# Delta-rule sequences of a hybrid decoder trunk: state maps made ahead of the chunk chain

## The chip, the cores and the metric

The kernel runs on one core of a Trainium2 chip. Its measure is the device time of one execution in microseconds (us), lower being better. The profile comes from one execution taken by the hardware profiler. Engines are named PE (TensorE, the matrix products), DVE (VectorE), ACT (ScalarE), POOL (GpSimd) and SP (SyncE, which here only issues DMAs).

## What is computed

The reference is a trunk of four layers over 1024 tokens of width 1024. Layers 0 and 3 are gated convolutions, layer 1 is a diagonal state-space layer, layer 2 is RWKV-7 time mixing. Each is followed by a gate and a layer norm. The change touches only layer 2, whose recurrence over time is, for each of 16 heads with a 64 x 64 state:

```python
def _rwkv_step(state, inp):
    r_t, w_t, k_t, v_t, kk_t, a_t = inp
    sa = jnp.einsum("bhvk,bhk->bhv", state, -kk_t)
    state = (state * w_t[:, :, None, :] + sa[..., None] * (kk_t * a_t)[:, :, None, :]
             + v_t[..., None] * k_t[:, :, None, :])
    out = jnp.einsum("bhvk,bhk->bhv", state, r_t)
    return state, out
# then: group norm of out over each head, times lnx_g plus lnx_b,
# plus a bonus sum(r*k*r_k)*v, times silu(z), times w_out
```

## The kernel before

All tensors of layer 2 lie transposed, 128 channels (two heads) on the partitions, and time is cut into two halves `h` of 512 tokens, each half into 8 chunks of 64. A block `m` (0 to 7) is one pair of heads. `rwkv_layer` runs, for each half, the z and v projections of all blocks, and then a loop over `m` (L1832 to L1863) that holds the recurrence in its chunked form. A projection of 512 columns is `mm3`: 24 products of 128x128 by 512 (L326 to L328).

The iteration of block `m` is made of generators of `inner_setup`: `use_k` and `use_r` (the scaled vectors: `kb` on the one side, `ra` on the other, `ant` the transposed half of `ra`, all per chunk), `prep` (the chunk-internal products, L1982, masked; `kb` scaled and transposed to `kbt`, L2001 to L2009; a product `wps` with v, L2017), `tsolve` (the triangular inverse on DVE, L2037 to L2054), `join` (its 32-blocks are put together to `tt`, L2063 to L2087, and applied to `ant`, L2097) and `seq` (the chain over the 8 chunks, and then norm and output).

In `seq`, `bank` (L2117 to L2123) first adds the v part of two chunk pairs into a PSUM bank `p1`. Then each chunk takes four steps that hang on each other: a PE product of `ra` with the state into `p1` (L2131), an ACT copy of the 64 result rows to `uv` (L2132), a PE product of `kbt` with `uv` into `p2` (L2137), and two DVE operations of 64x64 which decay the state and add the two diagonal blocks of `p2` (L2140). After chunks 3 and 7 the outputs are finished (L2147, L2150). The state is 128x128 with two 64x64 blocks in use. The norm (eight ACT squares L2162, POOL L2163 and L2169), four transposes back `otp` (L2176) and the last two POOL products (L2180, L2181) end `seq`.

Some 18 PSUM tiles per block rotate through `aux`, a pool of two banks. `p1` has two banks, `sq` (for `p2` and `otp`) one. Tiles from `slot(S, tag, ...)` share 16 buffers per tag: in the second half `tt`, `ant`, `uv`, two `scr` and two `kbt` of each block come from one such set.

What is issued when: the program is traced in the order of the generators' pulls (`pull(inner, IP)` takes `seq` of the block before last in pieces), and a scheduler then orders each engine's instructions by priority. `prio` moves `join` and `prep` ahead by 600 and `seq` and `tsolve` by 300. `issue_after(x)` keeps the PE instructions of a block behind `x`. Each engine then runs its list in that fixed order.

Of the kernel before, what the change touches and what calls it, by code (L numbers as in the profile page):

```python
# [15 lines left out]
P = 128  # L16
# [1527 lines left out]
PS, PT, PJ = 300, 300, 600  # L1544

# [52 lines left out]
def rwkv_layer(S, X, bg, l, last, nxt):  # L1598
# [9 lines left out]
    dST = dram_list(S, "dST", [P, P])  # L1608
# [182 lines left out]
    for h in range(2):  # L1791
# [38 lines left out]
        with S.tc.issue_after(act_set.ins):  # L1830
            Rs = [Ctx() for _ in range(NB)]
            for m in range(NB):  # L1832
# [47 lines left out]
            inner.append(prio(I.seq(NB - 1, h, Rs[NB - 1], dVT, dST, dBV, dZ, dY), PS))  # L1880
# [41 lines left out]
def inner_setup(S, rg, T_):  # L1922
# [35 lines left out]
    G.memset(zero, 0.0)  # L1958

    def prep(m, h, R):  # L1960
# [41 lines left out]
        R.kbt = []  # L2002
        for g in range(2):
            ps = aux("kbtp")
            for i in range(4):
                nc.tensor.transpose(ps[:, i * P:(i + 1) * P], kb[:, 4 * g + i, :], S.ident)
            t = slot(S, ("a0", "a1")[h], "kbt")
            SC.copy(t, ps)
            R.kbt.append(t.rearrange("p (a b) -> p a b", a=4))  # L2009
            yield  # L2010

        pss = [aux("wps"), aux("wps")]
        for c in range(4):
            for hd in range(2):
                for w in range(2):
                    rb, rk = rows_b[w], rows_k[w]
                    nc.tensor.matmul(pss[w][rb, c * P + hd * 64:c * P + hd * 64 + 64], sca[rk, w, c, hd, :],  # L2017
                                     R.uv[w][rk, c, hd * 64:hd * 64 + 64], start=True, stop=True)
# [3 lines left out]
        yield  # L2022

# [33 lines left out]
    def join(m, h, R):  # L2057
# [24 lines left out]
        for e in range(8):  # L2082
            for w in range(2):
                nc.tensor.matmul(ps[w][q0[w], e * 32:(e + 1) * 32], zs[q1[w], e, :], tt[q1[w], e, 32:64],
                                 start=True, stop=True)
# [6 lines left out]
        ps = [aux("a2"), aux("a2")]  # L2092
        for c2 in range(4):
            for hd in range(2):
                for w in range(2):
                    rb = rows_b[w]
                    nc.tensor.matmul(ps[w][hd * 64:hd * 64 + 64, c2 * CH:(c2 + 1) * CH],  # L2097
                                     an[rb, c2, hd * 64:hd * 64 + 64], tt[rb, 2 * c2 + hd, :], start=True, stop=True)
        for w in range(2):
            SC.copy(r5[:, :, w, acol[w]], ps[w][:, 0:256].rearrange("p (c t) -> p c t", c=4))  # L2100
# [4 lines left out]
    def seq(m, h, R, dVT, dST, dBV, dZ, dY):  # L2105
        st = rg.tile([P, P], F32, tag="state", name="state", bufs=2)
        if h == 0:
            G.memset(st, 0.0)
        else:
            nc.sync.dma_start(st, dST[m][:])  # L2110
        ot = rg.tile([P, HT], F32, tag="o", name="o", bufs=2)
        o4 = ot.rearrange("p (c s) -> p c s", c=4)

        def bank(ph):

            p1 = S.pseq.tile([P, 2, 2, P], F32, tag="p1", name="p1", bufs=2)
            nc.tensor.matmul(p1[:, 0, 0, 0:2], S.ident, zero, start=True, stop=False, skip_group_check=True)  # L2117
            for c2 in range(2):
                for hd in range(2):
                    for w in range(2):  # L2120
                        rb, cs = rows_b[w], slice(hd * 64, hd * 64 + 64)
                        nc.tensor.matmul(p1[rb, w, c2, cs], R.tt[rb, 2 * (2 * ph + c2) + hd, :],
                                         R.uv[w][rb, 2 * ph + c2, cs], start=False, stop=False, skip_group_check=True)  # L2123
            return p1
        p1s = [bank(0)]
        for c in range(8):
            w, c2, ph = c % 2, c // 2, c // 4
            rb = rows_b[w]
            uv = R.uv[w][:, c2, :]
            p1 = p1s[ph][:, w, c2 % 2, :]  # L2130
# [3 lines left out]
            if c == 2:  # L2134
                p1s.append(bank(1))
            p2 = sq("p2")
            last = nc.tensor.matmul(p2[:, 0:P], R.kbt[c // 4][:, c % 4, :], uv, start=True, stop=True)  # L2137
            for hd in range(2):
                cs = slice(hd * 64, hd * 64 + 64)
                V.scalar_tensor_tensor(st[cs, cs], st[cs, cs], R.pc[cs, c:c + 1], p2[cs, cs], ALU.mult, ALU.add)  # L2140
            if c % 4 == 3:
                with S.tc.issue_after(last.ins):
                    for k in range(2):
                        for hd in range(2):
                            for w in range(2):
                                cs = slice(hd * 64, hd * 64 + 64)
                                nc.tensor.matmul(p1s[ph][rows_k[w], w, k, cs], R.scr[w][:, 2 * ph + k, hd, :],  # L2147
                                                 R.uv[w][:, 2 * ph + k, cs], start=False, stop=True, skip_group_check=True)
                for w in range(2):
                    SC.copy(o4[rows_k[w], 2 * ph:2 * ph + 2, :], p1s[ph][rows_k[w], w])  # L2150
            yield
        if h == 0:
            nc.sync.dma_start(dST[m][:], st)
# [59 lines left out]
```

## Time and profile before

| | |
|---|---|
| time, median of 3 runs | 2817.57 us (2812.04 to 2817.90) |
| profiled execution | 2819.03 us, its span 2817.1 us |
| mean granted PE clock | 0.966 |
| PE, DVE, ACT, POOL busy | 95%, 71%, 41%, 23% of the span |

The shares are means over very different stages. The loop over the blocks of layer 2 lies, for the first half, from about 1290 to 1620 us after the span's start, and for the second from about 1745 to 2020 us; the chain of the last block of each half runs on into the stage behind it. In those stretches an engine's row in a timeline shows each instruction's start, its duration and, in brackets, the idle time before it with the engine and tile that ended it. Durations of PE rows overlap, since matmuls are pipelined: what one costs is read from start to start.

### The profile page before, as it was taken

What the parts mean: (1) busy time and instruction counts of PE and PEld (TensorE: products, weight loads), DVE (VectorE), ACT (ScalarE), POOL (GpSimd) and SP (SyncE); (2) the same over time, 40 slices, a digit from 0 to 9 for tenths busy, and PEclk for the clock granted to TensorE, in tenths of its full rate; (3) what the DMA queues carried; (4) which work ended last, traced back from release to release, by engine and by line L of the source; (5) the groups of instructions that cost most, each with busy time, mean ns of one, the idle gap of its engine ahead of it and who ended that gap; (6) DMA issues with size and microseconds to landing.
All of it is one profiled execution on the core that took longest, in us unless ns stands there. A gap on an engine that the chain in (4) does not pass through costs nothing.

```text
span 2817.1 us, 40692 instructions
## 1 busy us (share of the span) xinstructions
PE 2673.0 (95%) x14939; PEld 2119.2 (75%) x14939; DVE 2009.8 (71%) x3584; ACT 1168.8 (41%) x2243; POOL 644.9 (23%) x696
## 2 busy tenths in 40 slices
PE   8999999999999999899899899888889999999998
PEld 6887888778887878677677567666668777887887
DVE  6787865477657446887887776888866678877544
ACT  3333332242135223666565475555433343224332
POOL 1143422221115132203243110333222211111000
PEclk9999999999999999999996799999799999999999
DMA  5333321347774233473222245223324433324511
GB/s 169 99 97 98 94 76 58 92 146 211 217 237 157 90 101 102 134 227 120 77 95 91 60 163 168 76 85 93 100 91 135 139 115 116 101 72 131 172 64 38
DMA packets 463129, 331.56 MB, mean 118 GB/s; under 512 B 49449, under 2 KB 398929, under 8 KB 462929
## 3 DMA queue, kind: packets, MB, share of 16 engines
q1 hardware_dynamic: 462928, 328.96, 38.5%
q8 instruction: 118, 1.93, 0.3%
q14 instruction: 83, 0.67, 0.1%
HBM read 250.77 MB, written 77.59 MB: 117 GB/s over the span
## 4 chain that ended last, share of the span: by engine, by line
PE 71%; DVE 15%; issue 4%; ACT 4%; DMA 3%; POOL 3%; SPq 0%; DVEq 0%; POOLq 0%; ACTq 0%
PE op L327 3%; PE op L326 3%; PE op L328 3%; PE gp L328 3%; PE gp L327 3%; PE gp L326 3%; PE sp L326 2%; PE sp L327 2%; PE sp L328 2%; PE qa L506 2%; PE qa L507 2%; PE qa L508 2%; DVE tv L2048 2%; PE zp L326 2%; PE zp L328 2%
## 5 line engine op out<-in xcount | busy, mean ns | idle before, releaser
L299 DVE TENSOR_TENSOR wl<-wraw,wh 128x1024 fp32r<-128x1024 f32 x255 | 332.6, 1304 | 217.0 <-ACT wh L298 213.5
L298 ACT CAST wh<-wraw 128x1024 fp32r<-128x1024 f32 x255 | 267.4, 1049 | 519.0 <-PE gp L327 185.9
L905 POOL TENSOR_TENSOR ln_s<-ln_s,rp 128x512 f32<-128x512 f32 x42 | 60.3, 1435 | 209.9 <-DVE rp L901 209.9
L2140 DVE SCALAR_TENSOR_TENSOR state<-state,pc,p 64x64 f32<-64x64 f32 x256 | 70.8, 277 | 39.7 <-PE p L2137 35.5
L2048 DVE TENSOR_TENSOR tv<-ti,mi 128x128 f32<-128x128 f32 (+3 forms) x128 | 97.1, 759 | 2.5
L2131 PE MATMUL p<-state,ra 128*128 128x128 f32 x256 | 65.2, 341 | 31.3 <-DVE state L2140 31.0
L2131 PEld LDWEIGHTS p<-state,ra 128*128 128x128 f32 x256 | 45.2, 213 | 54.8 <-DVE state L2140 49.2
L2132 ACT COPY uv<-p 64x128 f32<-64x128 f32 x128 | 33.3, 260 | 122.2 <-PE p L2131 121.0
L920 POOL TENSOR_TENSOR rp<-r_0h,r_0l 128x512 f32<-128x512 f32 x24 | 36.5, 1548 | 180.9 <-PE op L327 180.2
L328 PE MATMUL gp<-r_0h,wl 128*128 128x512 f32 x192 | 77.2, 402 | 0.0
L327 PE MATMUL gp<-r_0l,wh 128*128 128x512 f32 x192 | 76.8, 400 | 0.0
L326 PE MATMUL gp<-r_0h,wh 128*128 128x512 f32 x192 | 76.6, 399 | 0.0
L326 PE MATMUL gp<-r_1h,wh 128*128 128x512 f32 x192 | 76.4, 398 | 0.0
L328 PE MATMUL gp<-r_1h,wl 128*128 128x512 f32 x192 | 76.0, 396 | 0.2 <-DVE wl L299 0.2
L327 PE MATMUL gp<-r_1l,wh 128*128 128x512 f32 x192 | 75.5, 393 | 0.0
L2137 PE MATMUL p<-uv,kbt 128*128 128x128 f32 x256 | 66.2, 344 | 8.7 <-ACT uv L2132 8.6
L1982 PE MATMUL s<-ra,kb 64*128 64x128 f32 x512 | 71.6, 302 | 1.0 <-ACT scr L1988 0.9
L2137 PEld LDWEIGHTS p<-uv,kbt 128*128 128x128 f32 x256 | 44.9, 210 | 36.6 <-ACT uv L2132 31.3
L1982 PEld LDWEIGHTS s<-ra,kb 64*128 64x128 f32 x512 | 61.3, 202 | 13.4 <-ACT scr L1988 2.9
L1991 POOL TENSOR_TENSOR scr<-scr,mask 128x512 f32<-128x512 f32 x32 | 45.9, 1435 | 70.2 <-ACT scr L1988 70.0
L327 PE MATMUL sp<-xs0l,wh 128*128 128x512 f32 x128 | 55.0, 430 | 1.9 <-DVE xs0l L195 1.9
L1710 POOL COPY pc<-pt 128x8 f32<-128x8 f32 x16 | 5.5, 342 | 222.0 <-ACT pt L1707 222.0
(851 smaller groups left out, 8734.7 us busy)
## 6 DMA issues: line engine op xcount, KB each, us to landing
wraw<-in_conv_w_in_dram SPq DMA_DIRECT2D x84, 512.0 KB
wraw<-in_rwkv_w_rkvz_dram SPq DMA_DIRECT2D x64, 512.0 KB
wraw<-in_ple_gate_dram SPq DMA_DIRECT2D x56, 512.0 KB
wraw<-in_conv_w_out_dram SPq DMA_DIRECT2D x24, 512.0 KB
xt<-xd SPq DMA_DIRECT2D x48, 256.0 KB
wraw<-in_ssm_w_in_dram SPq DMA_DIRECT2D x21, 512.0 KB
xd<-rp SPq DMA_DIRECT2D x40, 256.0 KB
wraw<-in_rwkv_w_out_dram SPq DMA_DIRECT2D x16, 512.0 KB
```

Of the source, the lines that this page charges most:

```text
L298: nc.scalar.copy(wh, raw)
L299: nc.vector.tensor_tensor(wl, raw, f32(wh[:]), ALU.subtract)
L326: nc.tensor.matmul(ps, lh, xh, start=(n == 0), stop=False)
L327: nc.tensor.matmul(ps, lh, xl, start=False, stop=False)
L328: nc.tensor.matmul(ps, ll, xh, start=False, stop=(n == kt - 1))
L506: nc.tensor.matmul(ps, wh[:, k0 + k, :], xh, start=first and k == 0, stop=False, skip_group_check=True)
L905: nc.gpsimd.tensor_tensor(s, s, rs, ALU.add)
L1982: nc.tensor.matmul(pss[hd][:, c * P:(c + 1) * P], kb[rows, 2 * c + w, :], ra[rows, 2 * c + w, :], start=True, stop=True)
L2048: V.tensor_tensor(tv, ti[:, b:8, 4 * b:4 * b + 4].unsqueeze(2).to_broadcast([P, n, c, 4]), mi[:, 4 * b:4 * b + 4, 0:c].rearrange("p q c -> ...
L2131: nc.tensor.matmul(p1, R.ra[:, c, :], st, start=False, stop=False, skip_group_check=True)
L2137: last = nc.tensor.matmul(p2[:, 0:P], R.kbt[c // 4][:, c % 4, :], uv, start=True, stop=True)
L2140: V.scalar_tensor_tensor(st[cs, cs], st[cs, cs], R.pc[cs, c:c + 1], p2[cs, cs], ALU.mult, ALU.add)
```

## The change

Only layer 2's `prep`, `join`, `seq` and the way they are queued are changed.

- `join` makes, besides the `ra` columns, `at` (16 products of 64x64 with an ACT copy) and from it, with `kbt`, a map `G` per chunk, written by 4 ACT copies into the diagonal blocks of a zeroed 128x128 tile (`gbd`, two buffers).
- `seq` makes both `p1` banks at once, copies them to `uv`, adds `kbt`·`uv` for all chunks into one bank `pd` (16 products of 128x64), and then a chunk's step is one PE product of `G` with the state (now 128x64) and one DVE operation. The states of all chunks are kept; `diag` spreads four of them into a block-diagonal tile, and `queries`, `to_uv` and `outs` make the outputs of four chunks together. In the second half the last step is left out.
- The squares of the norm become one ACT operation and one DVE reduction. The norm is a generator `tail` of its own.
- The transposes back and what follows are a generator `back`, traced one block later, without raised priority, its transposes (now in `aux`) kept behind the PE products of the next `join`.
- In `prep`, the transposes to `kbt` come behind the `wps` products.

```diff
@@ rwkv_layer, in the loop over m (and the same after it for the last block)
                 if m > 0:
                     for _ in prio(I.join(m - 1, h, Rs[m - 1]), PJ):
                         pass
-                    inner.append(prio(I.seq(m - 1, h, Rs[m - 1], dVT, dST, dBV, dZ, dY), PS))
+                    if m > 1:
+                        inner.append(I.back(m - 2, h, Rs[m - 2], dBV, dZ, dY, Rs[m - 1].joined))
+                    inner.append(prio(I.seq(m - 1, h, Rs[m - 1], dST), PS))
+                    inner.append(prio(I.tail(m - 1, Rs[m - 1]), PS))
@@ prep: kbt behind wps
+            with S.tc.issue_after(last.ins):
+                for i in range(4):
+                    nc.tensor.transpose(ps[:, i * P:(i + 1) * P], kb[:, 4 * g + i, :], S.ident)
@@ join
+        R.joined = last.ins
+        with S.tc.issue_after(last.ins):
+            pa = aux("at")
+            for c2 in range(4):
+                for hd in range(2):
+                    for w in range(2):
+                        rb = rows_b[w]
+                        nc.tensor.matmul(pa[rb, c2 * P + hd * 64:c2 * P + hd * 64 + 64], tt[rb, 2 * c2 + hd, :],
+                                         an[rb, c2, heads[hd]], start=True, stop=True)
...
+        SC.copy(at.rearrange("p c s -> p (c s)"), pa)
...
+                    nc.tensor.matmul(pg[w][heads[hd], c2 * CH:(c2 + 1) * CH], at[rb, c2, heads[hd]],
+                                     R.kbt[c2 // 2][rb, (2 * c2 + w) % 4, heads[hd]], start=True, stop=True)
         for w in range(2):
+            for hd in range(2):
+                SC.copy(g5[heads[hd], :, w, heads[hd]], pg[w][heads[hd], 0:256].rearrange("p (c t) -> p c t", c=4))
@@ seq
+        pd = sq("pd")
+        clear(pd[:, 0:2])
         for c in range(8):
+            for hd in range(2):
+                nc.tensor.matmul(pd[heads[hd], c * CH:(c + 1) * CH], R.kbt[c // 4][:, c % 4, heads[hd]],
+                                 R.uv[c % 2][:, c // 2, heads[hd]], start=False, stop=False, skip_group_check=True)
...
+        def chain(c):
+            col = pd[:, c * CH:(c + 1) * CH]
+            nc.tensor.matmul(col, R.g[:, c, :], sv[:, c, :], start=False, stop=True, skip_group_check=True)
+            V.scalar_tensor_tensor(sv[:, (c + 1) % 8, :], sv[:, c, :], R.pc[:, c:c + 1], col, ALU.mult, ALU.add)
+
+        def diag(ph):
+            for hd in range(2):
+                SC.copy(sbd[heads[hd], :, heads[hd]], sv[heads[hd], 4 * ph:4 * ph + 4, :])
...
-            nc.tensor.matmul(p1, R.ra[:, c, :], st, start=False, stop=False, skip_group_check=True)
-            SC.copy(uv[rb, :], p1[rb, :])
-            last = nc.tensor.matmul(p2[:, 0:P], R.kbt[c // 4][:, c % 4, :], uv, start=True, stop=True)
-            for hd in range(2):
-                V.scalar_tensor_tensor(st[cs, cs], st[cs, cs], R.pc[cs, c:c + 1], p2[cs, cs], ALU.mult, ALU.add)
+        for c in range(8):
+            if c < 7 or h == 0:
+                chain(c)
+            if c == 3:
+                diag(0)
+            elif c == 4:
+                queries(0)
+            elif c == 5:
+                to_uv(0)
+            elif c == 6:
+                outs(0)
@@ tail, back
-        for g in range(8):
-            SC.activation(gsq[:, g, :], o[:, g, :], AF.Square, scale=0.125, accum_out=s2[:, g:g + 1])
+        SC.activation(gsq, o, AF.Square, scale=0.125)
+        V.tensor_reduce(s2, gsq, mybir.AxisListType.X, ALU.add)
-        ps = sq("otp")
+        ps = aux("otp")
+        with S.tc.issue_after(behind) if behind else ExitStack():
```

## Rows read from the trace of the kernel before

**Rows 1.** Busy time of one period: window, its length, then PE, PEld, DVE, ACT, POOL (instructions).
```profile
1897.20:1934.70 37.50, 32.45 (x341) 24.77 (x339) 33.70 (x77) 22.17 (x64) 13.98 (x14) 1.00 0.28 87
```
**Rows 2.** PE timeline and chain that ended last: a chain's first product, its last, the next chain's first.
```profile
1877.52 0.49 PE L2131 MATMUL p<-state,ra 128*128 128x128 f32 x2
...
1904.83 0.27 PE p L2131 x2
...
1915.03 0.49 PE L2131 MATMUL p<-state,ra 128*128 128x128 f32 x2
```
**Rows 3.** DVE timeline: the first operation of the next join.
```profile
1868.86 1.09 DVE L2063 STREAM_TRANSPOSE tt<-ti 128x256 f32<-128x256 f32 x2
```
**Rows 4.** What PE waited for, 1820 to 1960 us: total us, times, longest.
```profile
PE p L2131 <- DVE state L2140: 11.2, 8, 2.1
PE otp L2176 <- POOL o L2169: 3.8, 4, 1.0
PE kbtp L2006 <- POOL kb L2001: 3.5, 3, 1.2
```
**Rows 5.** PE timeline: pairs and small tiles between the projections.
```profile
1867.18 0.38 PE L2131 MATMUL p<-state,ra 128*128 128x128 f32 x2
1867.32 0.47 PE L326 MATMUL sp<-xs1h,wh 128*128 128x512 f32 x1
1867.63 0.39 PE L327 MATMUL sp<-xs1l,wh 128*128 128x512 f32 x1
1867.91 0.49 PE L2137 MATMUL p<-uv,kbt 128*128 128x128 f32 x2
1868.33 0.69 PE L2147 MATMUL p<-uv,scr 128*64 128x64 f32 x16
1868.94 0.50 PE L328 MATMUL sp<-xs1h,wl 128*128 128x512 f32 x1
1869.28 0.39 PE L326 MATMUL sp<-xs1h,wh 128*128 128x512 f32 x1
1869.51 0.39 PE L327 MATMUL sp<-xs1l,wh 128*128 128x512 f32 x1
...
1911.76 0.73 PE L2097 MATMUL a<-tt,ant 64*64 64x64 f32 x31
...
1912.33 0.80 PE L2122 MATMUL p<-uv,tt 64*64 64x64 f32 x21
```
**Rows 6.** Groups by line: busy us, mean ns (L1693 instead: ns min/median/max).
```profile
L2140 DVE SCALAR_TENSOR_TENSOR state<-state,pc,p 64x64 f32<-64x64 f32 x58 | 15.9, 274 | 3.5 <-PE p L2137 2.9
...
L1693 DVE TENSOR_REDUCE vsum<-vt x16: 683/692/693, 1236.3 to 1733.8; 128x8 f32<-128x512 f32 x16
...
L2132 ACT COPY uv<-p 64x128 f32<-64x128 f32 x30 | 7.8, 259 | 35.3 <-PE p L2131 35.1
L2162 ACT ACTIVATE gsq<-o 128x64 f32<-128x64 f32 x28 | 6.9, 247 | 0.1
L2150 ACT COPY o<-p 64x256 f32<-64x256 f32 x14 | 5.1, 367 | 2.4 <-PE p L2147 2.2
...
L2008 ACT COPY kbt<-kbtp 128x512 f32<-128x512 f32 x8 | 4.3, 590 | 2.3 <-PE kbtp L2006 2.3
```
**Rows 7.** What the SP queue waited for, 1820 to 1960 us.
```profile
SPq L2171 <- POOL yt L2180: 5.1, 4, 1.3
```
**Rows 8.** End of the first half: windows as in Rows 1, then PE's waits 1510 to 1670 us.
```profile
1580.00:1590.00 10.00, 6.14 (x85) 4.18 (x84) 8.93 (x23) 4.73 (x10) 2.75 (x2) 1.00 0.35 86
...
1610.00:1620.00 10.00, 10.00 (x88) 5.62 (x88) 1.13 (x3) 4.46 (x18) 0.24 (x1) 0.50 0.16 41
...
PE p L2131 <- DVE state L2140: 8.6, 9, 2.6
PE p L2137 <- ACT uv L2132: 6.4, 12, 1.6
```
**Rows 9.** PE's longest wait at the end of layer 2, 2040 to 2180 us.
```profile
PE otp L2176 <- POOL u L528: 8.0, 1, 8.0
```

More of the change, by code (lines that the diff above doesn't have):

```diff
@@ L1879, in rwkv_layer @@
                 pass
-            inner.append(prio(I.seq(NB - 1, h, Rs[NB - 1], dVT, dST, dBV, dZ, dY), PS))
+            inner.append(I.back(NB - 2, h, Rs[NB - 2], dBV, dZ, dY, Rs[NB - 1].joined))
+            inner.append(prio(I.seq(NB - 1, h, Rs[NB - 1], dST), PS))
+            inner.append(prio(I.tail(NB - 1, Rs[NB - 1]), PS))
+            inner.append(I.back(NB - 1, h, Rs[NB - 1], dBV, dZ, dY, None))
     def resid(r, m, h, ps):
@@ L1958, in inner_setup @@
     G.memset(zero, 0.0)
+    heads = [slice(hd * 64, hd * 64 + 64) for hd in range(2)]
+    gbd = [rg.tile([P, 8, P], F32, tag=f"gbd{i}", name=f"gbd{i}") for i in range(GB)]
+    sbd = rg.tile([P, 4, P], F32, tag="sbd", name="sbd")
+    for t in (*gbd, sbd):
+        G.memset(t, 0.0)
     def prep(m, h, R):
@@ L2022, in prep @@
         yield
+        R.kbt = []
+        for g in range(2):
+            ps = aux("kbtp")
+            with S.tc.issue_after(last.ins):
+                for i in range(4):
+                    nc.tensor.transpose(ps[:, i * P:(i + 1) * P], kb[:, 4 * g + i, :], S.ident)
+            t = slot(S, ("a0", "a1")[h], "kbt")
+            SC.copy(t, ps)
+            R.kbt.append(t.rearrange("p (a b) -> p a b", a=4))
+            yield
     def tsolve(R):
@@ L2083, in join @@
             for w in range(2):
[L2084 to L2085 removed]
+                last = nc.tensor.matmul(ps[w][q0[w], e * 32:(e + 1) * 32], zs[q1[w], e, :], tt[q1[w], e, 32:64],
+                                        start=True, stop=True)
         for w in range(2):
@@ L2101, in join, with seq, clear @@
         yield
     gn, bn = S.vec[("lnx_g",)], S.vec[("lnx_b",)]
-    def seq(m, h, R, dVT, dST, dBV, dZ, dY):
-        st = rg.tile([P, P], F32, tag="state", name="state", bufs=2)
+    def seq(m, h, R, dST):
+        sv = rg.tile([P, 8, CH], F32, tag="state", name="state", bufs=SVB)
         if h == 0:
-            G.memset(st, 0.0)
+            G.memset(sv[:, 0, :], 0.0)
         else:
[L2110 to L2114, printed above, removed]
+            nc.sync.dma_start(sv[:, 0, :], dST[m][:])
+        R.ot = rg.tile([P, HT], F32, tag="o", name="o", bufs=1)
+        o4 = R.ot.rearrange("p (c s) -> p c s", c=4)
+        def clear(cols):
+            nc.tensor.matmul(cols, S.ident, zero, start=True, stop=False, skip_group_check=True)
+        p1s = []
+        for ph in range(2):
@@ L2152, in seq, with to_uv @@
-        if h == 0:
-            nc.sync.dma_start(dST[m][:], st)
-        hs = slice(h * HT, (h + 1) * HT)
+                        rb = rows_b[w]
+                        nc.tensor.matmul(p1[rb, w, k, heads[hd]], R.tt[rb, 2 * (2 * ph + k) + hd, :],
+                                         R.uv[w][rb, 2 * ph + k, heads[hd]], start=False, stop=False, skip_group_check=True)
+            p1s.append(p1)
+        def to_uv(ph):
+            for w in range(2):
+                SC.copy(R.uv[w][rows_b[w], 2 * ph:2 * ph + 2, :], p1s[ph][rows_b[w], w])
@@ new lines, in seq, with tail @@
+        for c in range(8):
[9 more added lines that the diff above has]
+                outs(0)
+            yield
+        diag(1)
+        if h == 0:
+            nc.sync.dma_start(dST[m][:], sv[:, 0, :])
+        queries(1)
+        to_uv(1)
+        yield
+        outs(1)
+        yield
+    def tail(m, R):
+        ot = R.ot
@@ L2169, in seq, with back @@
         G.tensor_tensor(o, o, bcs(s1), ALU.mult)
+        yield
+    def back(m, h, R, dBV, dZ, dY, behind):
+        ot, hs = R.ot, slice(h * HT, (h + 1) * HT)
         bv = S.tmp.tile([P, HT], F32, tag="ln_s", name="bv", bufs=1)
@@ L2183, in seq @@
         yield
-    I.prep, I.tsolve, I.join, I.seq = prep, tsolve, join, seq
+    I.prep, I.tsolve, I.join, I.seq, I.tail, I.back = prep, tsolve, join, seq, tail, back
     return I
```

81 lines of the change are left out of this document (37 added, 44 removed).

## The prediction, made before the changed kernel ran

> **What bounds the kernel now.** I read the page's 40 slices first, to find layer 2; then the windows table over single periods of its loop, the timelines of PE and DVE in one of them, the waits of PE, and the chain that ended last. In the middle of the second half the loop repeats itself every 37.5 us. In such a period no engine is full: PE is busy 32.45 us and DVE 33.7 us of 37.5, ACT 22.2 and POOL 14.0 [rows 1]. So neither engine's work alone sets the period. The chain does. Its first product starts at 1877.52 and its eighth at 1904.83; the next chain begins at 1915.03, 37.51 us after the first [rows 2]. That makes 27.3 us for seven steps (3.9 us each) and 10.2 us from the last product to the next chain's first, in which the next `join` runs. One period earlier it is the same: the last L2131 starts at 1867.18, the last L2137 at 1867.91, and the join's first DVE operation at 1868.86 [rows 3, 5]. The join follows the end of the previous chain because of buffers: its `tt` comes from 16 slots shared with the `kbt` of three blocks, and the last L2137 is what still reads one. So chain and join form a loop: chain, `kbt` free, join, next chain. What PE loses in it stands in its waits over 140 us, that is 3.73 periods: 11.2 us before L2131 for the state, 3.8 before the transposes back, 3.5 before the transposes of `kb` [rows 4]; per period 3.0, 1.0 and 0.94, together 4.95, which with 32.45 busy gives 37.4.
>
> **The change, part by part, for one period.**
>
> *The loop is cut.* `kbt` is read by `pd` at the start of `seq` and not at each step, so its slots are free a chain earlier and `join` no longer waits for the chain's end. A step loses an ACT copy (259 ns), one PE pair and one of two DVE operations (274 ns) [rows 6]. I therefore take the 37.5 us loop to go, and ask what the engines' own work allows then.
>
> *PE work.* A product here is two instructions. A pair among projections costs between 0.14 us (1867.18 to 1867.32) plus the 0.08 by which the next projection product comes later (0.31 instead of 0.23), that is 0.22, and 0.42 us ahead of a small-tile run (1867.91 to 1868.33) [rows 5]; I take 0.30, nearer the first since most pairs stand among projections. Small tiles: the 16 of L2147 take 0.61 us to the next start, 0.038 each; L2097, whose tiles alternate over all four quadrants, 0.57 us for 32 (1911.76 to 1912.33), 0.018 each; L2122, which uses two quadrants, 0.80 for 21, 0.038 [rows 5].
> - Removed: 8 pairs L2137, 8 x 0.30 = 2.4.
> - Kept: 8 pairs on `ra`, now in two runs of four at about 0.22 instead of 0.30 plus: -0.6, of which I count 0.3, because four pairs still stand at the ends of runs.
> - `at`: out rows and in rows belong to the same chunk parity, two quadrants as in L2122, 32 x 0.038 = 1.2. `gt`: four quadrants as in L2097, 0.57. `pd`: 32 of 128x64 as in L2147, 1.2. One more clearing product: at most a pair, 0.14.
> - `G` times the state: 8 pairs (7 in the second half) with 64 instead of 128 moving columns. The trace has no such form; it lies between two L2147 instructions (0.08) and a pair ahead of a switch (0.42). I take 0.26, 2.1 in all, nearer to the 128x128 pair because the weights are as wide.
> - Interruptions: a projection product after one is spaced 0.31 to 0.34 instead of 0.23 [rows 5]. Before, some 18 of them come from L2131, L2137 and L2147; after, some 12. Six times 0.08: -0.5.
>
> Sum: 1.2 + 0.57 + 1.2 + 0.14 + 2.1 - 2.4 - 0.3 - 0.5 = +2.0 us. PE has 34.45 us of work in a period.
>
> *DVE work.* Eight of sixteen state operations go, 8 x 0.274 = -2.2; one 128x512 reduction comes, 0.69 [rows 6]: -1.5, so 32.2 us. *ACT work.* Out: 8 copies of 0.26 and 8 squares of 0.25, -4.1. In: one 128x512 copy (0.59), one square taken at the same 0.59, and 4 + 8 + 4 copies of 64x256 for `gbd`, `to_uv` and `diag` at 0.37 [rows 6], +7.1. Net +3.0, 25.2 of 37.5: covered, but ACT's copies now stand inside `join`.
>
> *Waits of PE.* The 1.0 us before the transposes back goes: they come a join later, when their input is long done. The 0.94 before `kbt` goes: the `wps` run now stands in that gap. Of the 3.0 us before the chain's products I keep half: there are as many waits for DVE as before, behind the same DVE queue, but what PE waits for is one DVE operation instead of two, and the scheduler has more runs to put between. Bounds: 0 and 3.0. New: `at` and two `a2` want three tiles of a pool of two, and `gt` two more, so PE can stand behind an ACT copy twice; a copy is 0.37 to 0.59 and each comes with about as much of queue, so 0 to 1.8; I take 0.4, because the scheduler can fill the gap with projections.
>
> Period after: 34.45 + 1.5 + 0.4 = 36.3 us, 1.2 less. Of 16 blocks some 12 have a full period; 12 x 1.2 = -14 us.
>
> *What is moved.* `back` brings its two loads and its store on SP and two POOL products one block later. Their number stays; SP waits 5.1 us in four periods before these loads for their buffer [rows 7], behind which weight loads are queued, but these run two tiles ahead: no cost, or up to 1.3 us per block if a weight load comes late. `o` has one buffer instead of two; the next block's first output copy comes behind that `join` anyway.
>
> *End of the first half.* There the last tile solve and block 6's chain are nearly alone: PE is busy 6.14 of 10 us at 1580 and the clock is at half (0.50, that is 1.2 GHz) at 1610 [rows 8]. PE waits 8.6 us for the state and 6.4 us for `uv` between 1510 and 1670 [rows 8]. The second kind has no place in the new chain; of the first I keep half: -10.7. The 0.50 at 1610 to 1620, with PE busy all ten, would give back 5 us if the clock did not fall; it fell after the thin stretch. I count nothing for it, since the chain there stays latency-bound, and put it into the range.
>
> *End of layer 2.* The last block's transposes back hold PE for 8.0 us behind POOL [rows 9]. The chain ends earlier, but POOL's list is made by the scheduler: between 0 and -8, I take -5.
>
> Sum: -14 - 10.7 - 5 = -30 us against the profiled execution of 2819 us: 2789. The median of the runs shown is 1.5 us below that execution, so I say 2788.
>
> *A rule against it.* The projection product after an L2131 pair is late by 0.08 us although both are 128x128, and after the 128x64 run by 0.11 [rows 5]. The Trainium skill (TensorEngine Tiling (Array Packing), Key Properties) says that changing the tiling mode drains the engine, and that changing only the tile does not. By that, 128x128 pairs among 128x128 projections cost no drain, so gathering them saves nothing (the -0.5 falls), while `at`, `gt` and `pd` are three new runs with a switch at either end, 6 x 0.11 = 0.66. The row's 0.08 within one mode speaks against half of the rule; its 0.11 is in line with the other half.
>
> **The rivals.**
>
> *Small tiles pay at each switch.* By the same six switches of 0.11 and without the -0.5, PE has 35.6 us, the period is 37.5 and the 14 us fall: 2803. For it: the 0.11 is measured. Against it: `at` follows a small-tile run, so that some of the switches are shared.
>
> *PE becomes the bound and keeps its waits.* If the scheduler places each chain product as soon as its own model has the state ready, and DVE (33.7 of 37.5 busy) is later than that, PE stands at each of eight steps as it does now. Then the period is 34.45 + 3.0 + 1.8 = 39.25, 12 x 1.75 = +21; the end of the first half gives its 10.7, the end of the layer nothing: 2829. It decides against the change as soon as the waits left in a period pass 3.05 us. For it: DVE is nearly full, and its operations take their turn; the chain's waits are the largest item now. Against it: two of three items of wait are taken away by construction.
>
> *The loop isn't cut.* `seq` now takes both `p1` banks and the only `sq` bank from its start, so the next one can't begin before the last output copy. With step times near today's 3.9 us, 8 x 3.9 plus banks and outputs (about 6 us of runs and copies) is 37 us: the same period under another name. Only the ends then gain, and extra ACT work takes some back: 2814, between 2808 and 2820.
>
> *Resources alone.* If projections close up to 0.23, the waits fall under 1 us and the clock no longer drops: periods of 34.5, 12 x -3 = -36, ends -10.7 - 8, clock -6: 2758.
>
> **How the numbers follow.** Forecast (2775 to 2800): 0.36. Switches (about 2803): 0.12. Resources alone: 0.18. Loop not cut: 0.14, of which 0.04 is still faster. PE bound with its waits: 0.20. A measurement of this kernel tells 0.2% from no change, that is 5.6 us. Faster: 0.36 + 0.12 + 0.18 + 0.04 = 0.70. Same: 0.09. Slower: 0.21 with the loop's upper end. The range reaches from 2755, the last mentioned gain, to 2833, the slower rival with a margin; outside I leave 0.08 below and 0.08 above.
>
> **What would show it.** Right: in a period DVE's state operations number eight, PE's busy time rises to about 34 us, the waits before the transposes back and before `kbt` are gone, the chain's steps fall from 3.9 to 2 to 2.5 us, and `join` starts before the chain of the block before it has ended. Wrong: PE waiting 3 us or more for the new state operation or for the copies of `at` and `gt` (the slower rival); a new chain that begins right after the last output copy of the one before (loop not cut); projection products spaced as before (switches).

## The result, and the profile after

The changed kernel takes 2801.31 us (median of 15 runs, 2788.56 to 2808.62) beside 2815.30 us for the kernel before (15 runs, 2812.04 to 2820.98). The ratio is 0.9944 with an interval of 0.9929 to 0.9958: 14 us faster, where 30 were forecast. The profiled execution of after took 2808.62 us (span 2806.6, mean granted clock 0.976) and is the slowest of its 15; that of before took 2819.03 (span 2817.1, clock 0.966). The two spans are 10.5 us apart, and it is this difference that the traces have to explain.

**Where the time went, by landmarks.** The first join operation of block 0 and of block 7 in each half cuts both spans into the same five pieces. DVE timeline of before, then of after (start us, us, engine, line, operation):

```profile
1337.84 1.04 DVE L2063 STREAM_TRANSPOSE tt<-ti 128x256 f32<-128x256 f32 x2
...
2054.70 1.08 DVE L2063 STREAM_TRANSPOSE tt<-ti 128x256 f32<-128x256 f32 x2
```
```profile
1342.79 1.04 DVE L2077 STREAM_TRANSPOSE tt<-ti 128x256 f32<-128x256 f32 x2
...
2042.51 1.09 DVE L2077 STREAM_TRANSPOSE tt<-ti 128x256 f32<-128x256 f32 x2
```

The windows between these landmarks, of before and then of after, with the columns of [rows 1]: the loop of the first half, the piece between the halves, the loop of the second half.

```profile
1337.84:1604.25 266.41, 236.43 (x2195) 181.75 (x2195) 229.72 (x522) 150.72 (x420) 83.28 (x90) 0.86 0.27 83
1604.25:1794.24 189.99, 178.06 (x982) 133.29 (x982) 134.21 (x231) 118.07 (x232) 30.52 (x30) 0.92 0.44 140
1794.24:2054.70 260.46, 225.13 (x2224) 174.21 (x2225) 226.01 (x513) 143.36 (x408) 81.57 (x81) 0.91 0.30 90
```
```profile
1342.79:1597.86 255.07, 239.27 (x2901) 193.46 (x2901) 211.43 (x476) 172.06 (x388) 84.86 (x90) 0.95 0.29 85
1597.86:1794.08 196.22, 180.72 (x1059) 137.84 (x1060) 134.94 (x221) 120.17 (x217) 32.63 (x30) 0.93 0.44 138
1794.08:2042.51 248.43, 240.58 (x2864) 195.47 (x2864) 197.81 (x457) 162.32 (x370) 78.46 (x81) 0.92 0.28 88
```

The two loops gained 11.3 and 12.0 us. The rest lost: 5.0 before the first landmark (1337.84 to 1342.79), 6.2 between the halves, 1.7 after the last (762.4 to 764.1 us). The sum is -10.5, the difference of the spans.

The second half is the cleaner of the two, since its clock is nearly the same (0.91 and 0.92). PE's idle time there fell from 260.46 - 225.13 = 35.3 us to 248.43 - 240.58 = 7.9, and its busy time rose by 15.5: 27.5 less of waiting, paid for with 15.5 more of work. In the first half the clock rose from 0.86 to 0.95, so part of its 11.3 us is clock.

**Did a block get shorter?** The join changes its place within a block, so its landmarks can't tell. The transpose `mi`, the last DVE operation of `prep`, hangs on the same work of a block in both kernels. Windows from the `mi` of block 1 to that of block 7, six periods in each half, of before and then of after:

```profile
1330.87:1552.99 222.12, 203.11 (x1908) 158.50 (x1908) 191.58 (x433) 126.18 (x347) 77.29 (x81) 0.87 0.28 88
1787.34:2014.05 226.71, 195.29 (x1950) 152.26 (x1949) 196.65 (x440) 124.63 (x349) 78.04 (x77) 0.91 0.28 88
```
```profile
1334.87:1562.93 228.06, 214.50 (x2566) 174.00 (x2563) 185.56 (x423) 149.44 (x342) 81.16 (x85) 0.95 0.30 88
1786.05:2012.61 226.56, 219.15 (x2559) 178.37 (x2558) 180.44 (x412) 147.18 (x337) 76.75 (x79) 0.92 0.27 85
```

It did not. The twelve periods take 448.8 us before and 454.6 after. In the second half PE's idle time fell by 4.0 us a period (31.4 to 7.4 us in all) and its busy time rose by 4.0, so the mean period stays at 37.8. In the first half PE had only 3.2 us of idle time a period to lose, and 0.9 of it went. The whole gain lies around the periods: from block 7's `mi` of the first half to block 1's of the second, 234.4 us became 223.1, and from block 7's of the second to the end of the span 803.1 became 794.0. The start up to block 1 lost 4.0.

**One period.** Windows row of a period of after, against [rows 1]:

```profile
1897.00:1933.50 36.50, 35.75 (x436) 28.63 (x435) 28.39 (x68) 25.36 (x58) 13.06 (x15) 1.00 0.29 89
```

36.50 us against 37.50: PE is busy in all but 0.75. This period is at full clock; from `mi` to `mi` the six of the second half last 33.7 to 41.8 us. ACT is where the prediction put it (25.36, forecast 25.2), PE is over its forecast (35.75, forecast 34.45), DVE far under (28.39, forecast 32.2). PE timeline in it:

```profile
1903.05 1.08 PE L2113 MATMUL at<-ant,tt 64*64 64x64 f32 x29
...
1905.73 0.92 PE L2164 MATMUL p<-uv,tt 64*64 64x64 f32 x25
...
1907.27 0.68 PE L2134 MATMUL gt<-kbt,at 64*64 64x64 f32 x16 [0.62 <-ACT gbd L2138]
1907.93 0.34 PE L2179 MATMUL pd<-uv,kbt 128*64 128x64 f32 x4
...
1911.51 0.43 PE L2185 MATMUL pd<-state,gbd 128*128 128x64 f32 x2
...
1918.24 0.43 PE L2185 MATMUL pd<-state,gbd 128*128 128x64 f32 x2
```

Six chain steps take 6.73 us, 1.12 each, against 3.9 in [rows 2]; in the other chains of this half a step takes 1.1 to 1.8. The DVE timeline shows what the join follows instead:

```profile
1895.06 2.08 DVE L2012 STREAM_TRANSPOSE mi<-dg 128x1024 f32<-128x1024 f32 x1 [1.38 <-ACT dg L2008]
1897.05 1.09 DVE L2077 STREAM_TRANSPOSE tt<-ti 128x256 f32<-128x256 f32 x2
...
1931.57 2.06 DVE L2012 STREAM_TRANSPOSE mi<-dg 128x1024 f32<-128x1024 f32 x1 [1.38 <-ACT dg L2008]
1933.55 1.08 DVE L2077 STREAM_TRANSPOSE tt<-ti 128x256 f32<-128x256 f32 x2
```

Twice the join's `tt` follows the `mi` of the next block's `prep` at once, where in [rows 3] it came behind the end of a chain. Behind it stand the join's products, the chain and the next block's scores, whose diagonal blocks give the next `mi`. What PE waited for, 1820 to 1960 us as in [rows 4] (total us, times, longest):

```profile
PE pd L2185 <- DVE state L2186: 1.9, 1, 1.9
PE gt L2134 <- ACT gbd L2138: 1.8, 4, 0.6
```

18.5 us of waits have become 3.7. The waits of [rows 8] are gone alike: between 1500 and 1680 us PE waits for the state 1.3 us instead of 8.6, and the 8.0 of [rows 9] has become 0.7. A new one stands between the halves, before a projection product (PE's idle time in that whole piece rose from 11.9 to 15.5 us):

```profile
PE sp L326 <- DVE sg L1663: 5.3, 1, 5.3
```

**The clock.** Of one program, 15 runs of after lie between 0.976 and 0.986, and the time follows: a straight line through them falls 19.3 us per 0.01 of clock (correlation -0.97); 25 runs of before on one chip give 19.4 (-0.89), other sets of its runs 15 to 19. Before has a median clock of 0.968 to 0.970, after of 0.980. That difference by that slope is 19 to 23 us, more than the 14 won. At an equal clock of 0.975 the two lines give some 2803 us for before and 2812 for after. This is an estimate beyond the runs of either line (those 25 have clocks of 0.967 to 0.972, after's 0.976 to 0.986), and the granted clock is itself a consequence of what a kernel puts on PE; but it made a second question: did the maps gain the time, or the clock?

### The profile page after: what moved, and what is told of

Its sections match the earlier page's. It is cut to its first block, busy times and chain, and to the rows that moved or that the text cites. A ratio compares the mean times of both kernels' runs of the same rounds, so it can differ in the third digit from the quotient of the medians.

```text
span 2806.6 us, 43661 instructions
## 1 busy us (share of the span) xinstructions
PE 2709.2 (97%) x16491; PEld 2171.2 (77%) x16491; DVE 1961.2 (70%) x3464; ACT 1215.7 (43%) x2147; POOL 649.2 (23%) x699
## 4 chain that ended last, share of the span: by engine, by line
PE 75%; DVE 12%; issue 4%; ACT 4%; DMA 3%; POOL 1%; SPq 0%; DVEq 0%; ACTq 0%; POOLq 0%
PE op L327 4%; PE op L326 4%; PE op L328 4%; PE sp L327 3%; PE sp L326 3%; PE sp L328 3%; PE gp L328 3%; PE gp L327 3%; PE gp L326 3%; PE s L1995 2%; PE zp L326 2%; PE zp L327 2%; PE zp L328 2%; PE qa L507 2%; PE qa L506 2%
## 5 line engine op out<-in xcount | busy, mean ns | idle before, releaser
L326 PE MATMUL gp<-r_1h,wh 128*128 128x512 f32 x192 | 76.4, 398 | 0.0
L326 PE MATMUL gp<-r_0h,wh 128*128 128x512 f32 x192 | 76.0, 396 | 0.0
L2186 DVE SCALAR_TENSOR_TENSOR state<-state,pc,pd 128x64 f32<-128x64 f32 x120 | 33.3, 278 | 42.9 <-PE pd L2185 41.6
L2170 ACT COPY uv<-p 64x256 f32<-64x256 f32 x128 | 46.9, 367 | 31.7 <-PE p L2194 26.2
L2185 PEld LDWEIGHTS pd<-state,gbd 128*128 128x128 f32 x240 | 42.5, 207 | 21.8 <-DVE state L2186 12.4
L326 PE MATMUL sp<-xs3h,wh 128*128 128x512 f32 x128 | 52.6, 416 | 5.3 <-DVE sg L1663 5.3
L326 PE MATMUL sp<-xs0h,wh 128*128 128x512 f32 x128 | 56.6, 442 | 0.4 <-ACT xs0h L195 0.4
L2260 POOL TENSOR_TENSOR yt<-yt,bv 128x512 f32<-128x512 f32 x16 | 20.8, 1302 | 154.0 <-ACT yt L2259 110.5
L328 PE MATMUL sp<-xs0h,wl 128*128 128x512 f32 x128 | 55.7, 435 | 0.0
L195 ACT CAST r_0h<-r 128x512 fp32r<-128x512 f32 x32 | 19.9, 620 | 81.5 <-DVE r L406 39.4
```

Source lines behind the costliest of these rows:

```text
L326: nc.tensor.matmul(ps, lh, xh, start=(n == 0), stop=False)
L328: nc.tensor.matmul(ps, ll, xh, start=False, stop=(n == kt - 1))
L2170: SC.copy(R.uv[w][rows_b[w], 2 * ph:2 * ph + 2, :], p1s[ph][rows_b[w], w])
L2185: nc.tensor.matmul(col, R.g[:, c, :], sv[:, c, :], start=False, stop=True, skip_group_check=True)
```

## The experiments

The theory was that the chain and the buffers tied to it set the period before, and that PE's own work sets it after. Each median stands beside runs of before on the same chip, of which the ratio is formed. After itself was not run on the chips of e1 to e12, whose medians of before are 2813 to 2817 us, so a difference to after is good to a few us.

| run | us | ratio (interval) | clock, median |
|---|---|---|---|
| after | 2801.3 | 0.9944 (0.9929 to 0.9958) | 0.980 |
| e1 after, two products | 2820.1 | 1.0035 (1.0017 to 1.0052) | 0.956 |
| e2 before, two products | 2851.8 | 1.0141 (1.0126 to 1.0156) | 0.936 |
| e3 before, own buffers | 2827.4 | 1.0054 (1.0039 to 1.0069) | 0.964 |
| e4 after, two DVE steps | 2846.3 | 1.0112 (1.0074 to 1.0150) | 0.968 |
| e5 before, order parts only | 2820.3 | 1.0021 (1.0010 to 1.0031) | 0.963 |
| e6 after, back at once | 2912.4 | 1.0336 (1.0307 to 1.0364) | 0.952 |
| e7 after, kbt first | 2818.1 | 1.0005 (0.9995 to 1.0014) | 0.977 |
| e8 after, small chain | 2819.8 | 1.0008 (0.9993 to 1.0023) | 0.976 |
| e9 after, filler | 2819.4 | 1.0019 (1.0007 to 1.0030) | 0.977 |
| e10 before, filler | 2827.9 | 1.0041 (1.0028 to 1.0055) | 0.966 |
| e11 after, another order | 2821.8 | 1.0027 (1.0011 to 1.0042) | 0.974 |
| e12 before, fuller end | 2806.8 | 0.9975 (0.9963 to 0.9988) | 0.975 |

**e1 and e2: is PE's work the bound?** The third product of each `k` and `r` projection of the loop is left out (its low-order part is missing from the result): 256 products.

```diff
...
-        nc.tensor.matmul(ps, ll, xh, start=False, stop=(n == kt - 1))
+        if not two:
+            nc.tensor.matmul(ps, ll, xh, start=False, stop=(n == kt - 1))
```

> The changed kernel, with the third of the three products (L328) left out of the k and r projections of the loop, so that their low-order part is missing from the result: 16 blocks x 16 products, 256 in all, at 0.23 to 0.30 us from start to start, 59 to 77 us of PE work. Theory (PE's work is now what sets the period, 35.7 of 36.5 us busy): at least two thirds of it shows, 2740 to 2760 us against 2801. Rival (a loop of latencies through join and the two aux banks sets the period): less than 25 us, above 2776.

> The kernel before, with the same 256 products left out. Theory (its period is the chain plus join, not PE's work): the products lie beside the chain, only those in the join's 10 us shorten it, 10 to 30 us, 2785 to 2805 against 2815, clearly less than the changed kernel gains. Rival (PE's work set the period before as well): the same gain as in the changed kernel, 2755 to 2775.

Both came out slower than the kernel they were made from, after by 19 us, before by 39; e1 lies above 2776, where only the rival put it, and e2 where neither did. Windows of e1, three periods in a row from one `ra` of `prep` to the next, and of e2, 40 us each:

```profile
1838.80:1872.00 33.20, 32.27 (x404) 26.54 (x403) 26.19 (x64) 24.00 (x58) 14.40 (x15) 0.90 0.26 83
1872.00:1906.90 34.90, 33.27 (x424) 27.13 (x424) 32.02 (x69) 25.56 (x59) 14.23 (x14) 1.00 0.30 93
1906.90:1940.00 33.10, 30.74 (x401) 24.60 (x399) 29.17 (x67) 21.93 (x50) 12.85 (x13) 1.00 0.31 98
```
```profile
1850.00:1890.00 40.00, 35.99 (x321) 27.53 (x321) 32.95 (x71) 22.67 (x65) 14.69 (x14) 0.79 0.27 81
1890.00:1930.00 40.00, 35.89 (x321) 27.73 (x320) 33.34 (x75) 21.81 (x63) 13.80 (x14) 0.79 0.27 82
1930.00:1970.00 40.00, 35.88 (x321) 27.55 (x320) 33.40 (x75) 22.22 (x63) 13.82 (x14) 0.79 0.27 81
```

In e1 PE is busy 96.3 of these 101.2 us. From `mi` to `mi`, the four periods from 1835.08 to 1978.27 us last 35.8 in the mean, where after's four from 1820.79 to 1970.81 last 37.5; 16 products of 0.23 us would be 3.7. So PE's work bounds the period after, at least in part. The total still rose, because more of e1 ran at half clock: 249 us of the span in its profile, against 134 in after's. In e2 each 40 us had a stretch at half clock, and the mean of the six periods of the second half, 37.8 before, grew to 40.2. Short windows show only the levels 0.50 and 1.00 (1.2 and 2.4 GHz) and stretches that hold both; 0.79 is such a mixture. So work was taken from PE, the clock fell, and more was lost than saved. That the gaps which this opened are the cause is argued: in after the clock also falls where PE hardly waits (last section). The Trainium skill (TensorE: Matmul & The Clock Gate, "What's actually happening") says that the throttled state is the default and that activity releases it; the direction agrees with the rows of e1 and e2.

**e3: did the slots set the period before?** The kernel before, `tt` and `ant` in buffers of their own.

```diff
-        R.ant = slot(S, ("a0", "a1")[h], "ant")
+        R.ant = rg.tile([P, HT], F32, tag="antown", name="ant", bufs=2)
...
-        tt = slot(S, ("a0", "a1")[h], "tt")
+        tt = rg.tile([P, HT], F32, tag="ttown", name="tt", bufs=2)
```

> The kernel before, with tt and ant taken out of the shared 16 slots into two buffers each of their own. Nothing else changes. Theory (join waited for the chain's end because tt found no free slot): join moves ahead of the chain's end, the period falls from 37.5 towards 35 us, 2780 to 2800. Rival (the chain's own steps, one after the other, and the places DVE gives them set the period): within 6 us of 2815.

It took 12 to 14 us longer than before. DVE timeline of e3, joins and then the decay products `ra` of `prep`:

```profile
1836.17 1.10 DVE L2063 STREAM_TRANSPOSE tt<-ti 128x256 f32<-128x256 f32 x2
...
1868.20 1.12 DVE L2063 STREAM_TRANSPOSE tt<-ti 128x256 f32<-128x256 f32 x2
...
1899.05 1.09 DVE L2063 STREAM_TRANSPOSE tt<-ti 128x256 f32<-128x256 f32 x2
```
```profile
1838.96 0.69 DVE L1751 TENSOR_TENSOR ra<-sp,pt 128x512 f32<-128x512 f32 x1
...
1877.19 0.68 DVE L1751 TENSOR_TENSOR ra<-sp,pt 128x512 f32<-128x512 f32 x1
...
1916.52 0.69 DVE L1751 TENSOR_TENSOR ra<-sp,pt 128x512 f32<-128x512 f32 x1
```

The joins moved ahead (32 and 31 us apart in this stretch), so the slots had held them. But the blocks still go by at 38 and 39 us. From `mi` to `mi` the mean of six is 38.0 in the second half, 37.8 before. The slots set the join's place, not the period. The clock is lower too (0.964); there the line over the runs of before gives some 2825, so little is lost beyond what goes with the clock.

**e4: are the chain's steps still on the path after?** The new state operation in two halves of 64 partitions.

```diff
-            V.scalar_tensor_tensor(sv[:, (c + 1) % 8, :], sv[:, c, :], R.pc[:, c:c + 1], col, ALU.mult, ALU.add)
+            for hd in range(2):
+                hs_ = heads[hd]
+                V.scalar_tensor_tensor(sv[hs_, (c + 1) % 8, :], sv[hs_, c, :], R.pc[hs_, c:c + 1], col[hs_, :], ALU.mult, ALU.add)
```

> The changed kernel with each state step done by two 64-partition DVE operations instead of one, 0.28 us more latency and DVE time per step, 120 steps. Theory (the chain lies inside the period): within 8 us of 2801. Rival (the chain is still on the path): 120 x 0.28 = 34 us more, about 2835.

45 us slower than after. Fifteen more operations a block pair (8 and 7) in each of 8 pairs, at 0.274 us [rows 6], are 33 us. E4's clock is lower too (0.968 against 0.980); by the line over after's runs that is some 24 of the 45, which leaves some 20 of the 33. The chain is a good deal shorter but has not left the path.

**e5 to e7: the parts that only move work.** e5 is the kernel before with `back` deferred and `kbt` behind `wps`, without the maps. e6 is after with `back` in its old place; e7 is after with `kbt` ahead of `wps` again.

```diff
(e6)
-                    if m > 1:
-                        inner.append(I.back(m - 2, h, Rs[m - 2], dBV, dZ, dY, Rs[m - 1].joined))
+                    inner.append(prio(I.back(m - 1, h, Rs[m - 1], dBV, dZ, dY, None), PS))
(e7, the block moved ahead of the wps products)
-            with S.tc.issue_after(last.ins):
-                for i in range(4):
-                    nc.tensor.transpose(ps[:, i * P:(i + 1) * P], kb[:, 4 * g + i, :], S.ident)
+            for i in range(4):
+                nc.tensor.transpose(ps[:, i * P:(i + 1) * P], kb[:, 4 * g + i, :], S.ident)
```

> The kernel before with the two changes of order alone: the transposes back and what follows as a piece of their own, one block later and behind the next join's products, and the transposes to kbt behind the wps products. The chain and its products stay. Theory (the maps take the chain off the path, the order parts only fill PE's gaps; 1.0 and 0.94 us of wait per period go, and with fewer gaps the granted clock rises above 0.970): about half of the change's gain, 2800 to 2808. Rival 1 (the order parts are the whole gain, since maps cost PE as much as they save): 2795 or less. Rival 2 (chain and join are one loop, what PE waits for beside it doesn't matter): 2810 to 2818.

> The changed kernel with the transposes back queued right behind the block's own norm, at the raised priority, as before. Theory (PE waits for POOL again, 1.0 us in a period and up to 8 us at the end, and the gaps lower the clock): 2810 to 2825, clock under 0.978. Rival (nothing waits for them): 2795 to 2807.

> The changed kernel with the transposes to kbt ahead of the wps products again. Theory: 0.9 us of PE's wait per period comes back, 8 to 14 us, 2809 to 2815. Rival (kbt is now needed one join later only, PE finds other work): 2795 to 2807.

Without the maps the moves gain nothing (e5, 3 us over its runs of before); at e5's clock of 0.963 the line of before gives some 2827, so that a gain of some 7 may be hidden under the clock. Without the deferral the maps lose 111 us against after (e6). PE's waits in e6, 1340 to 1700 us:

```profile
PE otp L2254 <- POOL o L2241: 28.0, 7, 4.9
```

With the chain this short the output's norm is late for its own block: 4 us of waiting for each transposing back, where before it was 1.0 [rows 4]. In the second half another 17.2 us of it follow, and e6 is at half clock for 286 us against after's 134. The deferral is a condition of the maps. e7's +17 us looked like the price of the `kbt` order, until e11.

**e8: do 128x128 weights pay?** The chain's product as two 64x64 tiles per step.

```diff
-            nc.tensor.matmul(col, R.g[:, c, :], sv[:, c, :], start=False, stop=True, skip_group_check=True)
+            for hd in range(2):
+                hs_ = heads[hd]
+                nc.tensor.matmul(pd[hs_, c * CH:(c + 1) * CH], R.g[hs_, c, hs_], sv[hs_, c, :], start=False, stop=True, skip_group_check=True)
```

> The changed kernel with each state step done by 64x64 tiles, one per head, and not by one block-diagonal 128x128 product: four instructions instead of two. Theory (each step stands among 128x128 projections, so every small step pays two switches of about 0.1 us, 120 x 0.1 to 0.2): 12 to 24 us slower, 2813 to 2825. Rival (small tiles are cheaper, 4 x 0.018 to 0.038 instead of 0.25 us): 8 to 20 us faster, 2781 to 2793.

18 us slower than after, within what was expected, and no proof of it, as e11 shows.

**e9 and e10: can idle products hold the clock in the join?** Two idle 256-column products into unused columns, at three places of each join of after (e9) and of before (e10).

```diff
+    def fill(ps):
+        for _ in range(2):
+            nc.tensor.matmul(ps[:, 256:512].rearrange("p (a b) -> p a b", a=2), S.rw.ones_r, S.rw.ones_r.unsqueeze(1).to_broadcast([P, 2, P]), start=True, stop=True)
```

> The changed kernel with six idle products more per block (128x128 by 256 columns of a constant, into unused columns of the zp, tp and gt banks, never read): two behind each of these runs in join, 0.11 to 0.16 us each, 0.7 to 1.0 us per block, 11 to 16 us of PE work in all. Theory (the granted clock, which falls in the join's small-tile runs, is what the time hangs on): clock 0.984 or more, 2785 to 2798 in spite of the work. Rival (PE's work sets the time, the clock only follows): 2810 to 2818.

> The kernel before with the same six idle products per block, behind the zp, tp and a2 runs of join. Theory (clock): above 0.976 instead of 0.970, 2798 to 2810. Rival (work): 2820 to 2832, since the join is on its loop.

No: 18 us slower than after, and 12 us slower than before. The clock did not rise in either (0.977 against 0.980; 0.966 against 0.969), so the theory of both is out. How much of the 18 and the 12 us is the work of the products (11 to 16 us by their expectation) and how much the changed order, the runs don't separate.

**e11, a control: the same instructions in another order.** The planner's constant for the chain's priority is 280 instead of 300. No instruction is added or removed; some 600 of the 16491 products in PE's list stand elsewhere.

```diff
-PS, PT, PJ = 300, 300, 600
+PS, PT, PJ = 280, 300, 600
```

> A control: the changed kernel with the chain's priority raised by 280 instead of 300. Not an instruction is added or left out; the scheduler only places some of them elsewhere. It tells how much of a difference between two variants can be due to the order alone. Theory (the order of the lists matters little): 2795 to 2807. Rival (every other order costs, as the variants at 2818 to 2820 suggest, so that their differences can't be put down to their edits): 2812 to 2822.

2821.85 us: 20 us slower than after and slower than before. So the difference between after and before is smaller than what another order of after's own instructions makes, and the +17 to +19 of e1, e7, e8 and e9 can't be put down to their edits. By the lines over the clock, e11 has 2819 at 0.975, where after has 2812: some 7 of the 20 remain at equal clock, the rest goes with the clock (0.974 against 0.980).

**e12: idle work where PE is thin.** The kernel before, with a product by zeros added to each step of the `k` and `r` projections of blocks 6 and 7, ahead of the thin end of each half: 64 products, some 15 us of work that computes nothing.

```diff
...
+        if zw is not None:
+            nc.tensor.matmul(ps, zw, xh, start=False, stop=False)
```

> The kernel before with a fourth product of zero weights in the k and r projections of blocks 6 and 7 of each half, whose iterations hold the thin stretches with the clock at half: 64 products of 0.23 us, 15 us of idle work, the result unchanged. Theory (a fuller PE there keeps the clock up, which is how the changed kernel gains): clock 0.976 or more, 2800 to 2815. Rival (added work only costs): 2822 to 2832, clock at 0.970.

It is 7 us faster than before. Windows over the ends of the two halves, of before and then of e12:

```profile
1490.00:1640.00 150.00, 127.66 (x1035) 93.64 (x1034) 109.34 (x258) 84.42 (x235) 34.80 (x39) 0.73 0.26 80
1960.00:2110.00 150.00, 128.10 (x1054) 99.41 (x1053) 110.26 (x236) 69.25 (x205) 44.56 (x42) 0.84 0.30 93
```
```profile
1490.00:1640.00 150.00, 127.93 (x1077) 93.75 (x1073) 115.79 (x267) 89.28 (x244) 35.96 (x40) 0.84 0.31 92
1960.00:2110.00 150.00, 138.09 (x1093) 107.07 (x1094) 107.60 (x231) 72.26 (x203) 46.85 (x43) 0.91 0.33 100
```

The clock there rises from 0.73 to 0.84 and from 0.84 to 0.91, and half-clock time in the whole profile falls from 189 to 130 us. More work and less time can only come from the clock or from the order, which differs here as well; that the gain is accompanied by the higher clock speaks for the first, and e11 forbids calling it shown.

## Why the prediction was half right

The sign and the range held; the forecast of -30 was twice the -14 measured. The range (2755 to 2833) reaches over every rival as well, so that it held is worth little. The rival of the switches (2803, periods that gain nothing) came nearer than the forecast.

- **The loop of chain and join** is where the prediction failed. Step times, waits and the join's place all changed as said, but the -14 us of twelve shorter periods did not come: the twelve take 5.8 us more. What PE no longer waits for it spends on the maps' products (next two points). Of the 24.7 us priced for the loops (14 of periods, 10.7 of the first half's end) only the second came, as 11.2 from block 7's `mi` to block 1's of the second half, and from the last `mi` to the end 9.1 came where 5 were priced. So the sign is right by the ends of the halves, and in part by luck: the clock, counted at nothing, acts there too. Half-clock time in these two pieces fell from 44 to 24 and from 29 to 23 us, which by the 0.34 worked out below is some 7 and 2 us of the gain.
- **PE's work** was under-sized: +3.3 us in the period shown, not +2.0 (nearer +4, since the window of [rows 1] holds 51 projection products and after's 48; the mean of the second half's six is +4.0). This is the term that cancelled the gain. From 1903.05 to 1905.73 there stand 32 tiles of `at`, 32 of `a2`, 16 of `gt` and 5 of L2164: at the prices used (0.038 for `at` and L2164, 0.018 for the others) 2.27 us, and they took 2.68. The other 16 of `gt` took 0.66 (1907.27 to 1907.93), 0.041 each with the change to `pd`, where 0.018 was used: 0.37 more. `pd` took 1.5 instead of 1.2. Together +1.1 of the 1.3. The saving on interruptions came in good part: projection products that start 0.31 us or more behind the product before fell from 16 to 12, by 0.32 us instead of 0.5, and those that do so behind the chain's pairs from 9 (L2131, L2137) to 2 (L2185). So the rival of the switches had the right sum (+1.2) and only half of its mechanism: it took the saving away, which came, and what its 6 x 0.11 are of the 1.1 can't be separated from slower tiles. For the Trainium skill's rule (TensorEngine Tiling (Array Packing), Key Properties) the same holds: pairs gathered within one mode did save, against it; new runs did cost more than their tiles, in line with it.
- **PE's waits** that would be left were over-sized: 3.7 us over 140 us is 0.97 a period, not 1.9. Half of the state's waits was kept, 0.5 is left. But the 4.95 to start from was read in the second half and used for all twelve periods; in the first half PE is idle 3.2 us a period before and 2.3 after. The slower rival, which needed 3.05 a period, is out.
- **DVE** fell by 5.3 us in the period shown, not 1.5, and by 2.7 in the mean of six (196.65 to 180.44 us). Beside the eight state operations, some of its other operations became shorter (last section). The steps take 1.1 to 1.8 us and not 2 to 2.5; that DVE no longer delays them is the likely reason.
- **Outside the loops** the end of the layer was priced at -5 and everything else at 0; by the join's landmarks it came to +12.9 (5.0 + 6.2 + 1.7). Of the 5.0 before the loop, 3.6 are there already at an operation of the layer before (1119.64 against 1123.24 us), where no line of the change acts; up to there after's trace holds 17 us of half clock and before's 10. Between the halves stands the new wait of 5.3 for `sg`, a place that I never read. These landmarks also move work: between the last `mi` and the last join PE starts 29 products of L326 before and 17 after, so part of the loops' gain is only work that now comes behind them. The 8.0 us of [rows 9] vanished as said; what they are of the 9.1 from the last `mi` to the end can't be separated.
- **"What bounds" held one reading too many.** "The join follows the end of the previous chain because of buffers" is right (e3), but buffers weren't what made the period: freed of them, before goes no faster. That leaves the chain's steps, which no run shortened alone in before; e4 shows that they still count after.
- **"The clock counted at nothing"** was the second failed term. Half-clock time in the profiles fell from 189.2 to 133.6 us, by 56; 0.01 of clock is 56 us at half over a span of 2800 us, so the lines over the runs give 19.3 / 56 = 0.34 us for each, 19 us. Without that, the sum of the other terms would be about zero or slightly above.

What stays open: how much of the 14 us is the maps' and how much this order's. e11 has the maps and not the gain; e12 has half the gain and not the maps. Several orders of both kernels would be needed.

The kept traces settle a part of it. From block 7's `mi` of the first half to block 1's of the second, the kernels without the maps (before, e3, e5, e10, e12) take 227.6 to 234.4 us, of which 34 to 44 at half clock. Those with the maps (after, e6 to e9, e11) take 220.6 to 225.2, of which 24 to 34. E4 with its longer steps takes 237.4, and e1, with products left out, 230.3. So the maps shorten the end of the first half in each of these orders, and a part of it goes with the clock. The twelve periods take 444 to 466 us without the maps and 455 to 469 with them (e4 488, e6 569): these ranges overlap, and no shorter period can be seen.

## What to carry to other kernels

When PE is 95% busy and the clock has two levels, put the granted clock beside each time, and count what an edit does to it: products taken away went with a loss of 19 and 39 us here (e1, e2), idle ones in a thin end with a gain of 7 (e12), idle ones in the join with a loss of 18 and 12 (e9, e10). Before a difference of half a per cent is credited to an edit, run one reordering that changes nothing: here it moved 20 us. And judge a period's forecast by the mean of several, between landmarks that end the same work: the one period read here fell by 1.0 us, and the mean of six did not move. What was gained came at the ends of the halves, where the chain stands nearly alone.

## What the runs showed of the hardware that I had not expected

- The granted clock is no property of a program: after's 15 runs lie between 0.976 and 0.986, and 2808.6 to 2788.6 us go with them.
- With PE busy 35.9 of 40 us the clock of e2 was 0.79 in each of three windows in a row.
- The clock also falls where PE hardly waits. Over after's six periods of the second half PE is busy 219.15 of 226.56 us, and the clock is 0.92. From 1945.9 to 1952.8 us it is at half, though PE was idle for 0.7 us of the 14 before; it ran 32x32 and 64x64 tiles there, among projection products.
- A DVE operation can stretch while POOL works. In before, DVE timeline and POOL timeline, an operation of 128x72 takes 0.23 us, and another of the same size and line 1.42 while a POOL product of 1.89 us runs:

```profile
1922.76 0.23 DVE L2054 TENSOR_TENSOR ti<-ti,td 128x72 f32<-128x72 f32 x1
...
1931.28 1.42 DVE L2054 TENSOR_TENSOR ti<-ti,td 128x72 f32<-128x72 f32 x1
```
```profile
1930.71 1.89 POOL L2001 TENSOR_TENSOR kb<-kb,pc 128x1024 f32<-128x1024 f32 x1
```

In after's period all eight of them took 0.32 or less, and the group's mean fell from 432 to 227 ns, some 1.6 us of what DVE gained in that period; over the whole of both traces it fell from 394 to 324. The Trainium skill (SBUF — State Buffer, "SBUF: two separate sides") says that a DVE operation with two inputs in SBUF and a GpSimd one that reads SBUF shut each other out; the row agrees. Why they meet less after the change was not tried.
